# Two quarter products of a seven-product matrix multiply change places, in the MLPs of a transformer trunk

## The chip, the cores and the metric

The kernel runs on one core of a Trainium2 chip. The metric is the device time of one execution in microseconds (us). A core has five engines that work at the same time, each through its own queue of instructions in a fixed order, and that wait for one another by semaphores: TensorE (PE in the profile, with its weight loads shown as PEld), VectorE (DVE), ScalarE (ACT), GpSimd (POOL) and SyncE (SP, which issues nearly all of this kernel's loads).

## The reference

A trunk of two layers works on 512 tokens of width 1024, in float32. The first layer mixes tokens by stick-breaking attention beside a state-space model, the second by sparse attention. Behind each mixer stands an MLP with a residual and a layer norm, and only the two MLPs matter here:

```python
ALPHA = (2 * DEPTH) ** 0.25                      # DEPTH = 2
def sq_relu_mlp(x, w1, w2):                      # w1: 1024 x 4096, w2: 4096 x 1024
    return jnp.square(jax.nn.relu(x @ w1)) @ w2
x = layer_norm(ALPHA * x + sq_relu_mlp(x, mlp_w1[i], mlp_w2[i]), ln_ffn_g[i], ln_ffn_b[i])
```

## The kernel before

**Products of float32.** Each operand is split into a rounded part (`hi`, type fp32r, made by a cast on ACT) and the remainder (`lo`, made by a subtraction on DVE, for a few weights on POOL). Three matmuls, hi x hi, hi x lo and lo x hi, stand for one product of a 128 x 128 with a 128 x 512 piece.

**The MLP** (`mlp`, L205 to L271). Let h be the squared ReLU of x @ w1. It is made in blocks of 128 hidden columns, transposed, by `proj_fm` (L135): a load of 512 KB of w1 on SP, the cast L104 and the remainder L105 of these weights, 24 matmuls (L131 to L133), then on ACT the ReLU (L227) and the square (L228). Such a piece of work is called a w1 block here.

The product of h with w2 takes its 4096 hidden columns in four parts of 1024. The first three parts are the chunks; each is done by `down_chunk` (L273). The fourth part is done in the plain way (`mlp_block`). A chunk is a product of a 512 x 1024 matrix A (512 tokens by 1024 hidden columns of h) with a 1024 x 1024 matrix B (rows of w2). Each is cut in quarters. A11 and A21 are the first and the second 256 tokens of the chunk's first four h blocks (one tile, `hs[0]`), A12 and A22 those of its last four (`hs[1]`). B11, B12, B21 and B22 are 512 x 512 each, loaded from w2 as two pieces of 512 KB. Instead of eight quarter products the chunk makes seven, of sums and differences of quarters, in the manner of Strassen and Winograd; a quarter product's result goes by additions into one or more quarters of the residual x, or into a tile u that is added to three quarters at the end.

**One quarter product** (`product`, L302) takes two PSUM banks from a pool of four (`psb`). It makes the halves of its A operand (cast L298 on ACT, remainder L299 on DVE; tiles `whi` and `wlo` of the pool `self.wp`, which has four of each and shares them with the w1 blocks' weights), then of each of its two B pieces (L298, L299; `whi` and `wlo` of the MLP's own pool `hp`, four of each), and runs 24 matmuls (L311 to L313). Sums of B pieces are made by `combine` (L293, DVE), sums of A quarters by the lines L334, L345, L347 and L354 (DVE), results are added by L320 and L323 (DVE) or copied or added to u by L329 (ACT) and L331 (DVE).

**What stands between the products.** `down_chunk` is a generator. At each of its seven `yield`s the MLP issues one w1 block of the next chunk, and the eighth after the last. So in program order a w1 block follows each product, two of them stand at the end of a chunk, and the next chunk's first product comes right behind these two. The very first chunk of an MLP follows its own eight w1 blocks.

**What sets the order.** The program order is a wish. A planner simulates the program with estimated durations and writes each engine's queue from that; instructions whose operands are ready can pass others that wait. Buffers of a tag are handed out in rotation, and a load, a cast or a matmul that writes a buffer waits until the former tile in it has been read for the last time. Loads of B stand on SP's queue (L287) among those of the weights (L101).

**Names and lines of the steps below.** Before the change a chunk begins with the loads of B12 and B11, A21 + A22 (L334, written into A21), B12 - B11 (L293, written into B12), and the product of the two (L336), added to the quarters (1,1) and (0,1) of x. Then comes the w1 block, the loads of B22, and the product A11 x B11 (L341), added to the quarter (0,0) and gathered in u. Then follow (A12 - (A21 + A22 - A11)) x B22 (L348) and four more (L352, L356, L361, L363).

Of the kernel before, what the change touches and what calls it, by code (L numbers as in the profile page):

```python
# [11 lines left out]
ALU = mybir.AluOpType  # L12
# [23 lines left out]
class Trunk:  # L36
# [236 lines left out]
    def down_chunk(self, hp, w2, r0, hs, u, touched, last):  # L273

        nc, mm = self.nc, self.nc.tensor.matmul
        vec, act = nc.vector, nc.scalar
        a11, a21 = hs[0][:, :, 0:256], hs[0][:, :, 256:512]
        a12, a22 = hs[1][:, :, 0:256], hs[1][:, :, 256:512]  # L280

        def load(tag, j, n):
            ts = []
            for i in range(2):
                t = hp.tile([P, 1024], F32, tag=tag, bufs=2, name=self.nm(tag)).rearrange("p (k c) -> p k c", c=512)
                r = r0 + j * 512 + i * 256
                nc.sync.dma_start(t, w2[r:r + 256, n * 512:n * 512 + 512].rearrange("(k p) c -> p k c", p=P))  # L287
                ts.append(t)
            return ts

        def combine(out, x, y, op):
            for o, p, q in zip(out, x, y):
                vec.tensor_tensor(o, p, q, op)  # L293

        def halves(src, pool, c):
            hi = pool.tile([P, 1024], F32R, tag="whi", bufs=4, name=self.nm("whi")).rearrange("p (k c) -> p k c", c=c)
            lo = pool.tile([P, 1024], F32R, tag="wlo", bufs=4, name=self.nm("wlo")).rearrange("p (k c) -> p k c", c=c)
            act.copy(hi, src)  # L298
            vec.tensor_tensor(lo, src, hi.bitcast(F32), ALU.subtract)  # L299
            return hi, lo  # L300

        def product(a, b):  # L302
            pss = [self.psb.tile([P, 512], F32, tag="psb", name=self.nm("psb")) for _ in range(2)]
            ahi, alo = halves(a, self.wp, 256)
            for i in range(2):
                bhi, blo = halves(b[i], hp, 512)
                for t, ps in enumerate(pss):
                    tok = slice(t * P, (t + 1) * P)
                    for k in range(2):
                        lh, ll = ahi[:, 2 * i + k, tok], alo[:, 2 * i + k, tok]  # L310
                        mm(ps, lh, bhi[:, k, :], start=i + k == 0, stop=False)  # L311
                        mm(ps, lh, blo[:, k, :], start=False, stop=False)  # L312
                        mm(ps, ll, bhi[:, k, :], start=False, stop=i + k == 2)  # L313
            return pss

        def add(pss, row, col, op=ALU.add):
            for t, ps in enumerate(pss):
                xs = self.x[:, 2 * row + t, col * 512:col * 512 + 512]
                if (row, col, t) in touched:
                    vec.tensor_tensor(xs, xs, ps, op)  # L320
                else:
                    touched.add((row, col, t))
                    vec.scalar_tensor_tensor(xs, xs, ALPHA, ps, ALU.mult, op)  # L323

        def gather(pss):
            for t, ps in enumerate(pss):
                if ("u", t) not in touched:
                    touched.add(("u", t))
                    act.copy(u[:, t, :], ps)  # L329
                else:  # L330
                    vec.tensor_tensor(u[:, t, :], u[:, t, :], ps, ALU.add)  # L331

        b12, b11 = load("b12", 0, 1), load("b11", 0, 0)
        vec.tensor_tensor(a21, a21, a22, ALU.add)  # L334
        combine(b12, b12, b11, ALU.subtract)
        ps = product(a21, b12)  # L336
        add(ps, 1, 1)
        add(ps, 0, 1)
        yield
        b22 = load("b22", 1, 1)  # L340
        ps = product(a11, b11)  # L341
        add(ps, 0, 0)
        gather(ps)
        yield
        vec.tensor_tensor(a11, a21, a11, ALU.subtract)  # L345
        s4 = hp.tile([P, 4, 256], F32, tag="s4", bufs=1, name=self.nm("s4"))
        vec.tensor_tensor(s4, a12, a11, ALU.subtract)  # L347
        add(product(s4, b22), 0, 1)  # L348
        yield
        combine(b12, b22, b12, ALU.subtract)  # L350
        b21 = load("b21", 1, 0)
        gather(product(a11, b12))  # L352
        yield
        vec.tensor_tensor(a11, a22, a11, ALU.subtract)  # L354
        combine(b11, b12, b11, ALU.subtract)
        ps = product(a11, b11)  # L356
        add(ps, 1, 0)
        add(ps, 1, 1)
        yield
        combine(b22, b12, b21, ALU.subtract)  # L360
        add(product(a12, b21), 0, 0)  # L361
        yield
        add(product(a22, b22), 1, 0, ALU.subtract)  # L363
        if last:
            for row, col in ((0, 1), (1, 0), (1, 1)):
                xs = self.x[:, 2 * row:2 * row + 2, col * 512:col * 512 + 512]
                vec.tensor_tensor(xs, xs, u, ALU.add)
        yield
# [832 lines left out]
```

## Time and profile before

| | |
|---|---|
| median of 3 runs | 1206.27 us |
| lowest and highest run | 1199.74 and 1209.66 us |
| the profiled execution, its own time | 1203.52 us |
| its span, from first to last instruction | 1201.7 us |
| granted clock of TensorE, mean over the span | 0.972 of full |
| chunks of the first MLP (first matmul of each) | at 303.3, 391.5 and 479.9 us |
| chunks of the second MLP | at 891.4, 978.7 and 1067.0 us |

How to read the lines that follow. A group or a row names an engine, an operation and its line in the kernel, then the written tile, an arrow and the read tiles, shapes and a count (x6). Times are in us, in a timeline the first number is the start from the span's begin and the second the duration; square brackets hold the idle time of the engine just before and what ended it. `A <- B: 22.1, 6, 3.7` in a list of waits means that A waited for B for 22.1 us in all, in 6 places, the longest 3.7. Matmuls are pipelined: one starts before the modelled end of the one before it, so spacing is read from start to start. A chain of waits lists, going back from the end, what each step was released by; "issue" is a time in which nothing that the profile shows was waited for. The letter q behind an engine (SPq) is its sequencer, which issues loads. Several instructions of one group that follow each other are merged in one row with their count, whose duration then runs from the first to the last and includes what they waited.

### The profile page before, as it was taken

How to read it: one execution, taken by the hardware profiler on the slowest of the kernel's cores; microseconds unless marked ns; L12 is line 12 of the kernel's file. 1: busy time of each engine (PE TensorE's matmuls, PEld its weight loads, DVE VectorE, ACT ScalarE, POOL GpSimd, SP SyncE). 2: the span in 40 equal slices, each digit the busy share in tenths (PEclk: the TensorE clock that was granted, in tenths of full speed). 3: DMA queues.
4: the chain of work that ended last, by engine and by line, in shares of the span. 5: the costliest groups of instructions: out<-in, count | busy, mean ns of one | idle time of the engine just before them, and what ended most of it. 6: DMA issues, size and time to landing. Idle time of an engine off the chain costs nothing.

```text
span 1201.7 us, 15563 instructions
## 1 busy us (share of the span) xinstructions
PE 1125.3 (94%) x5860; PEld 934.5 (78%) x5860; DVE 842.7 (70%) x1255; ACT 533.6 (44%) x832; POOL 173.1 (14%) x201
## 2 busy tenths in 40 slices
PE   7989998999999998999999959998989989989997
PEld 6878776788787787888888847776978878878886
DVE  7997598673865865965568997549637667567736
ACT  5534486324543543554135437642334435445510
POOL 1044130410000000000021735324000000000001
PEclk9998999999899899999999979999999989999999
DMA  7535772930241341333056860034313414414101
GB/s 238 140 85 140 199 223 52 268 118 1 88 141 53 94 150 37 115 110 79 1 146 150 212 152 1 19 121 135 97 35 106 141 35 122 124 35 140 53 1 70
DMA packets 147306, 126.99 MB, mean 106 GB/s; under 512 B 24352, under 2 KB 115296, under 8 KB 147232
## 3 DMA queue, kind: packets, MB, share of 16 engines
q1 hardware_dynamic: 145552, 123.59, 36.1%
q10 hardware_dynamic: 1680, 2.41, 0.6%
q8 instruction: 46, 0.75, 0.3%
q14 instruction: 28, 0.23, 0.1%
HBM read 105.80 MB, written 5.37 MB: 93 GB/s over the span
## 4 chain that ended last, share of the span: by engine, by line
PE 77%; DVE 13%; DMA 4%; ACT 3%; issue 2%; SPq 1%; POOL 0%; POOLq 0%; DVEq 0%; ACTq 0%
PE psa L132 11%; PE psa L131 11%; PE psa L133 11%; PE psb L311 7%; PE psb L312 7%; PE psb L313 7%; PE pso L948 3%; PE psb L379 2%; PE psb L381 2%; PE psb L380 2%; PE pst L941 2%; DVE acc L1113 2%; DVE top L1112 2%; PE psb L840 2%; PE psb L842 1%
## 5 line engine op out<-in xcount | busy, mean ns | idle before, releaser
L132 PE MATMUL psa<-xlo,whi 128*128 128x512 f32 (+1 forms) x720 | 268.0, 373 | 0.0
L131 PE MATMUL psa<-xhi,whi 128*128 128x512 f32 (+1 forms) x720 | 267.0, 373 | 0.2 <-ACT xhi L202 0.2
L133 PE MATMUL psa<-xhi,wlo 128*128 128x512 f32 (+1 forms) x720 | 267.0, 371 | 0.0
L104 ACT CAST whi<-raw 128x1024 fp32r<-128x1024 f32 (+1 forms) x129 | 133.4, 1045 | 198.5 <-PE psa L132 115.0
L105 DVE TENSOR_TENSOR wlo<-raw,whi 128x1024 fp32r<-128x1024 f32 (+1 forms) x102 | 127.9, 1258 | 79.0 <-ACT whi L104 78.6
L311 PE MATMUL psb<-whi,whi 128*128 128x512 f32 x336 | 136.0, 405 | 22.1 <-ACT whi L298 22.1
L132 PEld LDWEIGHTS psa<-xlo,whi 128*128 128x128 f32 x720 | 136.5, 190 | 23.6 <-DVE xlo L203 0.4
L131 PEld LDWEIGHTS psa<-xhi,whi 128*128 128x128 f32 x720 | 135.8, 189 | 23.5 <-ACT xhi L202 0.5
L133 PEld LDWEIGHTS psa<-xhi,wlo 128*128 128x128 f32 x720 | 135.7, 188 | 23.1
L299 DVE TENSOR_TENSOR wlo<-b,whi 128x1024 fp32r<-128x1024 f32 x84 | 102.6, 1222 | 52.2 <-ACT whi L298 52.0
L312 PE MATMUL psb<-wlo,whi 128*128 128x512 f32 x336 | 134.8, 401 | 0.0
L313 PE MATMUL psb<-whi,wlo 128*128 128x512 f32 x336 | 133.1, 399 | 0.0
L298 ACT CAST whi<-b 128x1024 fp32r<-128x1024 f32 x84 | 88.4, 1052 | 55.8 <-PE psb L313 43.9
L311 PEld LDWEIGHTS psb<-whi,whi 128*128 128x128 f32 x336 | 66.0, 196 | 38.5 <-ACT whi L298 24.6
L105 POOL TENSOR_TENSOR wlo<-raw,whi 128x1024 fp32r<-128x1024 f32 x27 | 70.8, 2632 | 135.2 <-ACT whi L104 117.2
L184 POOL TENSOR_TENSOR rs<-rs,two 128x1 f32<-128x1 f32 x16 | 22.7, 1417 | 441.4 <-DVE rs L183 441.4
L313 PEld LDWEIGHTS psb<-whi,wlo 128*128 128x128 f32 x336 | 65.5, 195 | 14.3
L312 PEld LDWEIGHTS psb<-wlo,whi 128*128 128x128 f32 x336 | 65.7, 195 | 13.7
L293 DVE TENSOR_TENSOR b<-b,b 128x1024 f32<-128x1024 f32 x48 | 63.2, 1317 | 11.2 <-DMA b<-in_w_dram 10.3
L227 ACT ACTIVATE h<-psa 128x512 f32<-128x512 f32 x48 | 28.5, 594 | 80.6 <-PE psa L133 80.6
L334 DVE TENSOR_TENSOR h<-h,h 128x1024 f32<-128x1024 f32 x6 | 7.4, 1225 | 70.3 <-ACT h L228 70.3
L298 ACT CAST whi<-h 128x1024 fp32r<-128x1024 f32 x36 | 37.9, 1052 | 42.2 <-PE psb L312 34.4
(263 smaller groups left out, 2021.5 us busy)
## 6 DMA issues: line engine op xcount, KB each, us to landing
raw<-in_w_dram SPq DMA_DIRECT2D x80, 512.0 KB, 4.1
b<-in_w_dram SPq DMA_DIRECT2D x48, 512.0 KB, 4.4
raw<-in_w_in_dram SPq DMA_DIRECT2D x29, 512.0 KB, 4.4
raw<-in_w_out_dram SPq DMA_DIRECT2D x16, 512.0 KB, 4.9
qst<-hl SPq DMA_DIRECT2D x48, 128.0 KB, 3.8
kst<-hl SPq DMA_DIRECT2D x24, 256.0 KB, 4.5
gb<-in_ln_g_dram SPq DMA_DIRECT2D x4, 512.0 KB, 4.2
gb<-in_ln_b_dram SPq DMA_DIRECT2D x4, 512.0 KB, 5.1
```

What stands on the lines that cost most here:

```text
L104: nc.scalar.copy(hi[:, c], raw[:, c])
L105: (eng or nc.vector).tensor_tensor(lo[:, c], raw[:, c], hi[:, c].bitcast(F32), ALU.subtract)
L131: mm(ps, lhi, rhi, start=start, stop=False)
L132: mm(ps, lhi, rlo, start=False, stop=False)
L133: mm(ps, llo, rhi, start=False, stop=stop)
L293: vec.tensor_tensor(o, p, q, op)
L298: act.copy(hi, src)
L299: vec.tensor_tensor(lo, src, hi.bitcast(F32), ALU.subtract)
L311: mm(ps, lh, bhi[:, k, :], start=i + k == 0, stop=False)
L312: mm(ps, lh, blo[:, k, :], start=False, stop=False)
L313: mm(ps, ll, bhi[:, k, :], start=False, stop=i + k == 2)
L948: last = self.nc.tensor.matmul(po[64 * h:64 * h + 64, :], v[:, s, cols[h]:cols[h] + 64], wt[:, s, h, :], start=s == 0, stop=s == qb)
```

## The change

The product A11 x B11 comes first in each chunk: load of B11, product, addition, gathering, and the w1 block behind it. The load of B12, B12 - B11, A21 + A22, their product and its two additions follow as the second, with the w1 block behind them, and the load of B22 comes after that. All operands, all products and the other five products' order stay as they were.

```diff
-        b12, b11 = load("b12", 0, 1), load("b11", 0, 0)
+        b11 = load("b11", 0, 0)
+        ps = product(a11, b11)
+        add(ps, 0, 0)
+        gather(ps)
+        yield
+        b12 = load("b12", 0, 1)
+        combine(b12, b12, b11, ALU.subtract)
         vec.tensor_tensor(a21, a21, a22, ALU.add)
-        combine(b12, b12, b11, ALU.subtract)
         ps = product(a21, b12)
         add(ps, 1, 1)
         add(ps, 0, 1)
         yield
         b22 = load("b22", 1, 1)
-        ps = product(a11, b11)
-        add(ps, 0, 0)
-        gather(ps)
-        yield
         vec.tensor_tensor(a11, a21, a11, ALU.subtract)
         s4 = hp.tile([P, 4, 256], F32, tag="s4", bufs=1, name=self.nm("s4"))
         vec.tensor_tensor(s4, a12, a11, ALU.subtract)
```

## The prediction

> **What bounds the kernel now.** I began with the first part of the page, to see which engine fills the span.
>
> ```profile
> span 1201.7 us, 15563 instructions
> PE 1125.3 (94%) x5860; PEld 934.5 (78%) x5860; DVE 842.7 (70%) x1255; ACT 533.6 (44%) x832; POOL 173.1 (14%) x201
> ```
>
> PE is busy for 1125.3 of 1201.7 us. An order of work can win only what PE loses, which is its 76.4 us without a matmul and the time in which its matmuls run slowly. So the second view is the list of PE's waits, longest total first; this row is the top one.
>
> ```profile
> PE psb L311 <- ACT whi L298: 22.1, 6, 3.7
> ```
>
> L311 is the first matmul line of `product`, L298 the cast in `halves`. There are six waits for six chunks (three in each of the two MLPs), the longest 3.7 us, and 22.1/6 = 3.68, so all six are alike. The third view is the chain of waits around one of them, the second chunk of the first MLP.
>
> ```profile
> 387.55 0.24 PE psa L133
> 387.79 0.02 issue
> 387.81 0.61 ACT h L227
> 388.42 0.02 issue
> 388.44 0.64 ACT h L228
> 389.08 0.02 issue
> 389.10 1.24 DVE h L334
> 390.34 0.02 issue
> 390.36 1.05 ACT whi L298
> 391.41 0.04 issue
> 391.45 0.80 PE psb L311
> ```
>
> The last matmul of the w1 product (L133) ends; its block is rectified (L227) and squared (L228); then DVE forms A21+A22 (L334), ACT casts it (L298), and only then can the chunk's first product start. The last block of h is a part of A22, so this chain is real data dependence, with PE empty beside it. The fourth view, busy time by stretch, shows a second loss behind the pause. Columns: length, busy time of PE, PEld, DVE, ACT and POOL with counts, granted clock, DMA share, GB/s. The first six rows run from a chunk's first product matmul to the first matmul of its second product, 48 matmuls each (24 of the product, 24 of a w1 block; the count may be one off at an edge). The seventh is the next such pair.
>
> ```profile
> 303.28:316.89 13.61, 13.61 (x48) 11.00 (x49) 13.43 (x14) 5.85 (x6) 0.00 (x0) 0.80 0.27 77
> 391.45:405.31 13.86, 13.86 (x48) 11.23 (x49) 13.42 (x14) 5.85 (x6) 0.00 (x0) 0.78 0.26 76
> 479.88:492.29 12.41, 12.41 (x49) 10.17 (x50) 12.38 (x13) 5.85 (x6) 0.00 (x0) 0.88 0.30 86
> 891.42:904.08 12.66, 12.66 (x48) 10.17 (x49) 12.63 (x13) 5.84 (x6) 0.00 (x0) 0.87 0.30 84
> 978.65:992.45 13.80, 13.80 (x48) 11.17 (x49) 13.42 (x14) 5.85 (x6) 0.00 (x0) 0.78 0.27 76
> 1067.02:1079.64 12.62, 12.62 (x49) 10.33 (x50) 12.59 (x13) 5.85 (x6) 0.00 (x0) 0.88 0.29 83
> 316.89:327.77 10.88, 10.88 (x49) 9.01 (x48) 8.85 (x9) 6.23 (x9) 0.00 (x0) 1.00 0.41 114
> ```
>
> PE is busy all through these rows, yet the same 48 matmuls take 12.41 to 13.86 us behind a pause, at a granted clock of 0.78 to 0.88, and 10.88 us at clock 1.00, 0.227 us apiece. So each chunk loses twice: the pause, and the slow clock after it.
>
> **Part 1: A11 x B11 first, the gain.** What does the new first product need? The product reads A11 and B11. A11 is the first 256 tokens of the chunk's first four h blocks, so it waits for the fourth block, not the eighth. ACT's timeline shows both in the stretch that makes the second chunk's operands.
>
> ```profile
> 351.08 0.64 ACT L228 ACTIVATE h<-h 128x512 f32<-128x512 f32 x1
> ...
> 363.33 1.05 ACT L298 CAST whi<-b 128x1024 fp32r<-128x1024 f32 x1 [0.73 <-PE psb L313]
> 365.82 1.06 ACT L104 CAST whi<-raw 128x1024 fp32r<-128x1024 f32 x1 [1.44 <-PE psb L312]
> ```
>
> The fourth block is squared by 351.72, 36 us before the w1 products end. B's first piece for the coming product is cast at 363.33 already. The cast at 365.82, the weights of the chunk's last w1 block, waited for a matmul of the sixth product: the `whi` tag has four buffers in each pool, handed out in program order, so a cast waits for the last use of the tile four places back. For the first product's A, four places back are the weights of the w1 block that follows the sixth product, and 24 matmuls of 0.227 behind 365.8 those are free, at 371.3. The cast of A11 can thus run from there, 1.05 us as at 363.33, and its fp32r remainder behind it, done by 374, against 387.6 when PE wants them. B11 needs no subtraction, one step less than B12-B11, so its pieces are no later than those cast now.
>
> The pause then goes. Its price is start to start, because the ends of matmuls are modelled:
>
> ```profile
> 387.38 0.39 PE L133 MATMUL psa<-xhi,wlo 128*128 128x512 f32 x1
> 391.45 0.80 PE L311 MATMUL psb<-whi,whi 128*128 128x512 f32 x1 [3.68 <-ACT whi L298]
> ```
>
> 391.45 - 387.38 is 4.07; less one matmul of 0.227 it is 3.84 us, times six 23.1 us. The slow clock goes with it: the six rows sum to 78.96 us, and six at 10.88 make 65.28, so 13.7 us. Together **36.8 us**. Bounds: 23.1 if the slow clock somehow stayed, 36.8 if PE never pauses; I take the upper, since the clock is at 1.00 once PE has run on for a while (seventh row).
>
> **Part 2: A21+A22 and B12-B11 second, the new cover.** L334, the two L293 subtractions, the cast and remainder of A21 and the B12 halves now stand behind a product and a w1 block: 10.88 us of PE work. From the chain, the way from the last w1 matmul to the cast's end is 391.41 - 387.79 = 3.6 us, and the remainder, one more DVE pass over such a tile like L334 below, adds 1.2 us, 4.8 in all. So 6 us are spare, and I cost the move at nothing. If the cover were gone, the old 3.84 and its slow clock would be back.
>
> ```profile
> 340.35 1.23 DVE L293 TENSOR_TENSOR b<-b,b 128x1024 f32<-128x1024 f32 x1 [2.39 <-DMA b<-in_w_dram]
> 376.93 1.06 ACT L298 CAST whi<-b 128x1024 fp32r<-128x1024 f32 x1 [1.67 <-PE psb L313]
> 389.10 1.22 DVE L334 TENSOR_TENSOR h<-h,h 128x1024 f32<-128x1024 f32 x1 [7.85 <-ACT h L228]
> ```
>
> B12-B11 is finished at 341.6 now; the second product's last B piece is cast at 376.93, so this subtraction has 35 us to spare and may come one product later. DVE stands idle 7.85 us ahead of L334, behind which it then does the remainders of A21, of the next w1 weights and of A11. Of these, A11's and the weights' move into that idle time. ACT's two copies of the product into u (first chunk), DVE's two adds into x and two into u come 10.88 us earlier than they did; they read a finished product, and four banks serve two products, so none holds PE.
>
> Does the chunk as a whole still fit? This row is one chunk, from its first product to the next chunk's.
>
> ```profile
> 391.45:479.88 88.43, 84.74 (x361) 69.63 (x361) 60.22 (x62) 38.95 (x46) 0.00 (x0) 0.96 0.31 95
> ```
>
> 360 matmuls at 0.227 are 81.6 us; 60.22 us of DVE are 74% of that, 38.95 of ACT 48%. PE stays the bound.
>
> **Part 3: the loads.** B11's two loads come ahead of B12's, B12's move behind the first product and its w1 weights, B22's two move behind one more w1 weight load. All are on SP's queue. The landing time of such loads is the last number of the second fence, in us:
>
> ```profile
> 322.15 4.00 SPq L287 DMA_DIRECT2D b<-in_w_dram  x2
> 330.09 0.37 SPq L101 DMA_DIRECT2D raw<-in_w_dram  x1
> 333.03 4.00 SPq L287 DMA_DIRECT2D b<-in_w_dram  x2
> ...
> 354.79 5.03 SPq L287 DMA_DIRECT2D b<-in_w_dram  x2
> 362.72 45.96 SPq L101 DMA_DIRECT2D raw<-in_w_dram  x5
> ```
>
> ```profile
> b<-in_w_dram SPq DMA_DIRECT2D x48, 512.0 KB, 4.4
> ```
>
> In order, these are next chunk's B12, B11 and B22, each issued when its buffer came free. Even right behind the first issue of the 362.72 row B12 would be in by 362.7 + 0.4 + 4.4 = 367.5, some 30 us before its product. B22 in that place would be in as early, and its product, the third, starts two products and two w1 blocks after 387.6, at 409.4. I take nothing for the loads, with 0 and the wait of rival D as bounds.
>
> **Sum.** The profiled execution took 1203.5 us (span 1201.7 and 1.8 around it); less 36.8 it is 1166.7. The median of the runs, 1206.3, is 0.2% above the profiled one; from it the same gain gives 1169.5. I forecast **1168 us**.
>
> **Rivals.**
>
> A, the second product comes late: the DVE queue is the tightest near the chunk's start. In the second chunk's row it works 13.42 us where 10.88 will be there. If all of that had to be done before the third product, 2.54 us a chunk would stay, 15.2 in all: 1168 + 15 = 1183. For it: DVE is in order, and L345 and L347 queue there for the third product. Against: 7.85 us idle just ahead. Its pauses would be well below 3.68, and I add no slow clock, because a pause of 1.97 had none (clock 1.00 in the second row); with it the time would be 1183 + 13.7 = 1197.
>
> ```profile
> 245.75 1.09 PE L199 MATMUL pst<-ident,x 128*128 128x128 f32 x8 [1.97 <-DVE x L189]
> 243.00:250.00 7.00, 5.03 (x31) 4.20 (x29) 6.97 (x11) 3.56 (x6) 2.18 (x2) 1.00 0.00 0
> ```
>
> The page "TensorE: Matmul & The Clock Gate" of the Trainium skill, Part 1, states that an idle window of about 3.4 us halves the clock until PE has been busy for as long again. By that rule, too, pauses of 2.54 us would cost only themselves, 1183 and not 1197.
>
> B, the pause is a lack of buffers. Then the first product, whichever it is, gets its `whi` tile only when the last w1 block is done, the pause of 3.68 stays, and the time is 1204 to 1206. For it: casts do wait for buffers (365.82, above). Against: the chain shows no buffer, but L227, L228 and L334. The page "Perfetto Trace Analysis" of the Trainium skill, under the optimization strategy, says that one gap repeating on the busy engine can mean too little SBUF or PSUM; by that rule the order would win nothing. This trace speaks against it here.
>
> C, the change doesn't do what it says: a planner writes each engine's order from simulated times and may place the cast of A11 behind that of A21. No gain, 1204 to 1206. Against: it already hands out buffers in program order, and that order now has A11 first.
>
> D, slower: B12's loads come to stand behind all the weight loads that hold SP from 362.72 to 408.68. Then the second product starts at 408.7 + 4.4 + 1.2 (L293) + 1.1 (L298) = 415.4 instead of 387.6 + 10.9 = 398.5. That is 16.9 us, in the four chunks that are not loaded ahead, 67.6 us, and some 2.3 us of slow clock each: 1168 + 77 = 1245. The change is lost once wait and slow clock in each of the four pass 36.8/4 = 9.2 us. Against: every pair of b is issued ahead of that block, and B12's buffer is free first of all.
>
> **Numbers.** Forecast 0.80, A 0.09, B 0.04, C 0.03, D 0.04. Unknown in the forecast itself: the slow clock after equal pauses cost 1.5 to 3.0 us, so the kernel's other slow stretches may shift by a few us, and single runs of before lie from 6.5 below to 3.4 above the median. That makes 1158 to 1178, and with A the range is **1158 to 1184**, which leaves out B, C, D and the edges, some 0.15. A measurement tells 1% (12 us) from no change. Faster by over 1% are the forecast and A, 0.89; within 1% B and C, 0.07; slower D, 0.04.
>
> **What would show it.** PE's wait list has no row of L311 behind L298; the twin stretches behind the w1 blocks are 10.88 us at clock 1.00; A11's cast stands before the last L228 of its chunk; L334 runs beside the first product; chunks are 81.6 us apart. I am wrong if L311 waits at the second product's start (A, D), or if the first still waits behind L298 (B, C).

## The result, and the profile after

The changed kernel takes 1166.07 us in the median of four runs (1164.96 to 1169.02), the kernel before 1206.23 us beside it. The ratio is 0.9677, 95% interval 0.9632 to 0.9722: faster by 3.2%; the medians differ by 40 us. The forecast was 1168 us in a range of 1158 to 1184, with 0.89 for faster by over 1%.

First the page of the changed kernel, whose span is 38.2 us shorter.

```profile
span 1163.5 us, 15569 instructions
PE 1108.7 (95%) x5860; PEld 923.6 (79%) x5860; DVE 841.5 (72%) x1255; ACT 532.4 (46%) x832; POOL 173.1 (15%) x201
```

The engines do the same work; PE is busy for 16.6 us less with the same 5860 matmuls, since fewer of them run at the slow clock. Next, the top of PE's list of waits after.

```profile
PE psl L1136 <- DVE pst L1143: 14.6, 1, 14.6
PE psu L131 <- ACT whi L104: 6.9, 1, 6.9
```

The row of L311 behind L298, which led this list with 22.1 us, is gone, and no wait of the MLP's chunks has come in its place. Busy time by stretch shows the other loss: these are the first product and the w1 block behind it in the first MLP's three chunks, the twins of three of the six rows in the prediction (length; busy PE, PEld, DVE, ACT, POOL; clock).

```profile
299.31:310.19 10.88, 10.88 (x50) 9.01 (x49) 9.33 (x9) 7.18 (x10) 0.00 (x0) 1.00 0.00 0
380.91:391.79 10.88, 10.88 (x50) 9.01 (x49) 9.33 (x10) 6.21 (x8) 0.00 (x0) 1.00 0.00 0
462.51:473.39 10.88, 10.88 (x50) 9.01 (x49) 9.33 (x10) 6.21 (x8) 0.00 (x0) 1.00 0.00 0
```

Each takes 10.88 us at clock 1.00, as do the second MLP's three, and their starts are 81.6 us apart. Where did the 38.2 us come from? The same view by stage, first of the kernel before, then of the changed one: the first MLP from its w1 blocks to its fourth part, the attention between the MLPs, and the second MLP with the last normalisations ahead of it.

```profile
265.79:563.00 297.21, 286.16 (x1272) 237.26 (x1273) 194.62 (x198) 137.10 (x167) 0.53 (x1) 0.97 0.29 88
563.00:830.90 267.90, 245.50 (x1509) 202.75 (x1507) 194.63 (x450) 115.45 (x262) 95.21 (x113) 0.97 0.40 106
830.91:1150.14 319.23, 307.49 (x1425) 257.16 (x1425) 211.59 (x221) 144.85 (x176) 4.44 (x3) 0.97 0.28 84
```

```profile
265.65:544.11 278.46, 278.46 (x1273) 232.40 (x1274) 194.01 (x198) 136.72 (x167) 0.53 (x1) 1.00 0.31 94
544.11:810.40 266.29, 244.10 (x1510) 201.44 (x1508) 194.61 (x450) 115.44 (x262) 95.15 (x113) 0.97 0.39 107
810.38:1111.85 301.47, 300.78 (x1424) 253.22 (x1425) 210.95 (x221) 144.59 (x176) 4.44 (x3) 0.99 0.30 89
```

The two MLPs gave 18.75 and 17.76 us, 36.5 together, where 36.8 were forecast; in the first one PE is now busy for all of its 278.46 us. The attention gave 1.6 us that the change has nothing to do with. There a stretch at the slow clock is gone, before and after:

```profile
629.46 0.81 PE L1077 MATMUL psx<-kist,qist 96*128 96x256 f32 x3 [1.86 <-issue]
629.00:634.00 5.00, 4.54 (x25) 4.32 (x26) 3.10 (x6) 1.65 (x6) 0.00 (x0) 0.66 1.05 267
```

```profile
610.12 0.59 PE L1078 MATMUL psx<-kist,qist 96*128 96x256 f32 x3 [1.41 <-issue]
610.10:615.10 5.00, 4.99 (x40) 4.85 (x41) 3.28 (x7) 2.62 (x9) 0.00 (x0) 1.00 1.04 258
```

Last, how near the new cover is to its end. In the second chunk of the changed kernel these are ACT's and DVE's rows for A11 (first two), for the sum A21+A22 and its halves, and PE's row at the second product's start; the last w1 block's ReLU starts at 381.11.

```profile
364.56 1.05 ACT L298 CAST whi<-h 128x1024 fp32r<-128x1024 f32 x1 [3.43 <-PE psa L132]
365.65 1.23 DVE L299 TENSOR_TENSOR wlo<-h,whi 128x1024 fp32r<-128x1024 f32 x1 [3.08 <-ACT whi L298]
...
381.11 0.60 ACT L227 ACTIVATE h<-psa 128x512 f32<-128x512 f32 x1 [4.17 <-PE psa L133]
382.40 1.23 DVE L340 TENSOR_TENSOR h<-h,h 128x1024 f32<-128x1024 f32 x1 [4.33 <-ACT h L228]
383.82 1.05 ACT L298 CAST whi<-b 128x1024 fp32r<-128x1024 f32 x1 [1.46 <-PE psb L313]
384.79 1.05 ACT L298 CAST whi<-h 128x1024 fp32r<-128x1024 f32 x1
388.39 1.22 DVE L299 TENSOR_TENSOR wlo<-h,whi 128x1024 fp32r<-128x1024 f32 x1
391.79 0.39 PE L311 MATMUL psb<-whi,whi 128*128 128x512 f32 x1
```

A11 is cast 15 us and its remainder done 14 us ahead of the first product at 380.91, released by a w1 matmul as forecast. The sum's cast ends 4.7 us behind the last w1 matmul and its remainder 8.5 us behind it; the sum is ready at 383.63, then ACT casts a piece of B first, and from the end of the sum's cast (385.84) to 388.39 DVE does other things. That matters below.

### The profile page after: what moved, and what is told of

Its sections match the earlier page's. It is cut to its first block, busy times and chain, and to the rows that moved or that the text cites. A ratio compares the mean times of both kernels' runs of the same rounds, so it can differ in the third digit from the quotient of the medians.

```text
span 1163.5 us, 15569 instructions
## 1 busy us (share of the span) xinstructions
PE 1108.7 (95%) x5860; PEld 923.6 (79%) x5860; DVE 841.5 (72%) x1255; ACT 532.4 (46%) x832; POOL 173.1 (15%) x201
## 4 chain that ended last, share of the span: by engine, by line
PE 80%; DVE 12%; DMA 3%; issue 2%; ACT 2%; SPq 1%; POOLq 0%; DVEq 0%; ACTq 0%
PE psa L133 11%; PE psa L132 11%; PE psa L131 11%; PE psb L313 7%; PE psb L311 7%; PE psb L312 7%; PE pso L949 3%; PE psb L382 3%; PE psb L381 3%; PE psb L380 2%; PE pst L942 2%; DVE acc L1114 2%; DVE top L1113 2%; PE psb L841 2%; PE psb L842 2%
## 5 line engine op out<-in xcount | busy, mean ns | idle before, releaser
L133 PEld LDWEIGHTS psa<-xhi,wlo 128*128 128x128 f32 x720 | 135.8, 189 | 23.1
L131 PEld LDWEIGHTS psa<-xhi,whi 128*128 128x128 f32 x720 | 135.0, 188 | 23.1 <-ACT xhi L202 0.5
L299 DVE TENSOR_TENSOR wlo<-b,whi 128x1024 fp32r<-128x1024 f32 x84 | 102.5, 1221 | 43.0 <-ACT whi L298 42.8
L311 PE MATMUL psb<-whi,whi 128*128 128x512 f32 x336 | 130.7, 389 | 0.0
L312 PE MATMUL psb<-wlo,whi 128*128 128x512 f32 x336 | 130.7, 389 | 0.0
L313 PE MATMUL psb<-whi,wlo 128*128 128x512 f32 x336 | 129.7, 389 | 0.0
L298 ACT CAST whi<-b 128x1024 fp32r<-128x1024 f32 x84 | 88.3, 1051 | 42.0 <-PE psb L313 30.2
L312 PEld LDWEIGHTS psb<-wlo,whi 128*128 128x128 f32 x336 | 63.1, 188 | 13.2
L313 PEld LDWEIGHTS psb<-whi,wlo 128*128 128x128 f32 x336 | 63.1, 188 | 13.1
L311 PEld LDWEIGHTS psb<-whi,whi 128*128 128x128 f32 x336 | 63.1, 188 | 13.0
L298 ACT CAST whi<-h 128x1024 fp32r<-128x1024 f32 x36 | 38.0, 1054 | 54.0 <-PE psb L312 34.0
L299 DVE TENSOR_TENSOR wlo<-h,whi 128x1024 fp32r<-128x1024 f32 x36 | 43.9, 1220 | 14.0 <-ACT whi L298 13.5
L841 PE MATMUL psb<-whi,xhi 128*128 128x512 f32 x128 | 51.5, 410 | 0.8 <-DVE x L848 0.6
```

Source lines behind the costliest of these rows:

```text
L131: mm(ps, lhi, rhi, start=start, stop=False)
L133: mm(ps, llo, rhi, start=False, stop=stop)
L841: nc.tensor.matmul(ps, chi[:, k, tok], whi, start=i == 0, stop=False)
```

## The experiments

All ratios are to the kernel before, run on the same chip in the same job, with their 95% interval.

**The loads alone.** The new order of the loads with the old order of the products (B12 stays ahead of the first product, which needs it):

```diff
-        b12, b11 = load("b12", 0, 1), load("b11", 0, 0)
+        b11 = load("b11", 0, 0)
+        b12 = load("b12", 0, 1)
...
-        b22 = load("b22", 1, 1)
         ps = product(a11, b11)
         add(ps, 0, 0)
         gather(ps)
         yield
+        b22 = load("b22", 1, 1)
```

> The products keep the order of the kernel before; only the loads change as in the change (B11 ahead of B12, B22 behind the second product). My theory, that the whole gain is the pause before A21+A22 and the slow clock after it, expects no change: six waits of L311 behind L298 of 3.68 us each and 1200 to 1210 us. The rival, that a part of the gain comes from the other order of the loads, expects less than 1195 us.

Measured: 1204.0 us, ratio 1.000 (0.998 to 1.002). The wait is the old one, word for word:

```profile
PE psb L311 <- ACT whi L298: 22.1, 6, 3.7
```

So the order of the loads in the program neither gives nor takes anything. The traces say why. In the stretch that loads the second chunk, SP issues the four pairs of B pieces, the first piece of each within 0.1 us of the end of the remainder (L299) that reads its buffer last, at 322.15, 333.03, 343.92 and 354.79 us before, at 324.05, 334.93, 345.81 and 356.69 in this run, at 315.98, 326.32, 337.30 and 348.09 in the changed kernel. In all three they come in the order of the buffers, B12 first. The changed order of the program did not reach SP's queue there.

**The first MLP alone.** `down_chunk` takes the new order where `self.n_mlp == 1`, else the old one.

> The change is made in the first MLP alone. My theory adds up by chunks: three pauses of 3.84 us and the slow clock of those three chunks (2.73, 2.98 and 1.53 us) are 18.8 us, so about 1187 us, with three waits of L311 left, all behind 850 us of the span. The rival, that the chunks' gains depend on each other or come from elsewhere (the attention between the MLPs, the tail), expects 1168 or 1206 us, or three waits with a time off by more than 6 us.

Measured: 1184.4 us, ratio 0.9835 (0.981 to 0.986), 19.9 us by the ratio where 18.8 were expected. Three waits are left:

```profile
PE psb L311 <- ACT whi L298: 11.0, 3, 3.7
```

The gain adds up by chunks. One of the three pauses left, though as long as the others, has no slow clock behind it (more of that under the clock rule):

```profile
873.97:884.86 10.89, 10.89 (x48) 8.93 (x49) 10.86 (x11) 5.86 (x6) 0.00 (x0) 1.00 0.34 96
```

**The cover taken away.** A11 x B11 stays first, but one w1 block earlier, so that the product of the sums follows the chunk's last w1 block directly:

```diff
             for c in range(3):
-                ups = up_raw(c + 1) if c < 2 else itertools.chain(up_split(6), up_split(7))
-                got = []
-                for _ in self.down_chunk(hp, w2, c * 1024, hs, u, touched, c == 2):
+                down = self.down_chunk(hp, w2, c * 1024, got[-1], u, touched, c == 2)
+                next(down)
+                got += ups
+                ups = up_raw(c + 1) if c < 2 else itertools.chain(up_split(6), up_split(7))
+                got = []
+                for _ in down:
                     got += itertools.islice(ups, 1)
-                got += ups
-                hs = got[-1]
+                got += itertools.islice(ups, 1) if c < 2 else ups
```

(The first chunk's w1 blocks are issued up to the seventh ahead of the loop in the same way.)

> A11 x B11 is still first, but one w1 block earlier, ahead of the chunk's last w1 block, so that the product of the sums follows that block directly, as the first product did before the change. My theory, that the gain is the cover of 10.88 us between the last w1 block and the product of the sums, expects the pause of 3.84 us and the slow clock back six times, at the second product: 1200 to 1209 us. The rival, that A11 x B11 first is better in itself (fewer steps, earlier casts), expects 1163 to 1172 us.

Measured: 1203.9 us, ratio 0.9996 (0.998 to 1.001). PE waits as before, now at the second product (L313 is that kernel's number for L311, L300 for L298):

```profile
PE psb L313 <- ACT whi L300: 22.1, 6, 3.7
```

All of the gain is gone although A11 x B11 is still first and all buffers are the same. So what pays is the work that stands between the last w1 block and the product of the sums. This also settles rival B: with the same four buffers the pause comes and goes with the order alone.

**A shorter pause in the kernel before.** The sum in two instructions:

```diff
-        vec.tensor_tensor(a21, a21, a22, ALU.add)
+        for k in (slice(0, 3), slice(3, 4)):
+            vec.tensor_tensor(a21[:, k], a21[:, k], a22[:, k], ALU.add)
```

> The kernel before, with A21+A22 made in two instructions, three blocks of h and then the last one, so that only a quarter of the sum is left behind the last block. A 128x1024 pass takes 1.23 us and a 128x512 one 0.68, so a quarter should take about 0.4: the pause falls from 3.84 to about 3.0 us start to start, 5 us in six. If the slow clock needs an idle time of a full 3.4 us (the rule of the page), it goes as well, 13.7 us more: about 1187 us. If it needs only little activity over some window, it stays: about 1201 us. I hold the first for likelier.

Measured: 1195.3 us, ratio 0.9922 (0.989 to 0.995), between the two expectations. List of waits, then the stretches from the chunks' first product to their second:

```profile
PE psb L311 <- ACT whi L298: 17.3, 6, 2.9
```

```profile
302.79:315.14 12.35, 12.35 (x48) 10.13 (x49) 12.32 (x13) 5.84 (x6) 0.00 (x0) 0.88 0.30 85
388.90:399.94 11.04, 11.04 (x48) 9.04 (x49) 11.01 (x12) 5.87 (x6) 0.00 (x0) 1.00 0.34 95
...
1057.28:1071.22 13.94, 13.94 (x48) 11.21 (x49) 13.45 (x14) 5.84 (x6) 0.00 (x0) 0.78 0.26 75
```

All pauses are alike, 2.88 us. The clocks behind them are 0.88, 1.00 and 0.78 in the rows shown and 0.79, 0.87 and 1.00 in those left out. So an idle time shorter than 3.4 us can bring the slow clock, and whether it does changes from one equal pause to the next. The two effects are apart here: the pauses shrank by 22.1 - 17.3 = 4.8 us, the rest of the 9.4 us (0.78% of 1203.9) is slow clock that was spared.

**A longer pause in the kernel before.** Two more DVE passes behind the sum (A22 is subtracted and added again), 1.25 us each:

```diff
         vec.tensor_tensor(a21, a21, a22, ALU.add)
+        for _ in range(1):
+            vec.tensor_tensor(a21, a21, a22, ALU.subtract)
+            vec.tensor_tensor(a21, a21, a22, ALU.add)
```

> The kernel before with two more DVE passes behind A21+A22: each pause is 2.5 us longer, 6.2 instead of 3.68. If the slow clock's price belongs to the clock's return alone, as I hold, it stays at 1.5 to 3.0 us a pause and the time grows by the pauses only, six times 2.5 = 15 us: 1217 to 1223 us. If the price grows with the pause (2.3 us for 3.68, so 3.9 for 6.2), it is 10 us more: 1229 us or so.

Measured: 1221.2 us, ratio 1.0131 (1.011 to 1.015), 15.8 us more, with six waits of 6.2 us:

```profile
PE psb L311 <- ACT whi L298: 37.2, 6, 6.2
```

The pauses grew by 37.2 - 22.1 = 15.1 us, which leaves 0.7 for the slow clock, where the interval of the ratio is 2.8 us to either side. Its price belongs to each return, not to the length of the pause.

**Half the cover.** The first two products in a row, the two w1 blocks behind them:

```diff
         gather(ps)
-        yield
         b12 = load("b12", 0, 1)
...
         add(ps, 0, 1)
         yield
+        yield
         b22 = load("b22", 1, 1)
```

> The changed kernel without a w1 block between its first two products: both stand in a row, two w1 blocks behind them. The cover falls from 10.88 to 5.44 us. My theory says that the way to A21 takes 3.6 us to the end of the cast and 4.8 to the end of the remainder, both less than 5.44: no wait at the second product, 1163 to 1170 us. The rival A of the prediction, that DVE's queue is what limits the chunk's start, expects a pause of 1 us or more in each chunk, 1172 us or more.

Measured: 1177.7 us, ratio 0.977 (0.975 to 0.979). My theory said no wait, and there is one of about 1.15 us in four chunks (and of 0.55 in the two others, behind DVE's L299):

```profile
PE psb L311 <- ACT whi L298: 4.6, 4, 1.2
```

```profile
381.81:396.14 14.33, 13.17 (x57) 10.36 (x56) 12.78 (x13) 8.56 (x10) 0.00 (x0) 1.00 0.05 11
```

(The second is the stretch around such a wait; the clock stays at 1.00.) DVE's queue of this kernel says why:

```profile
383.30 1.23 DVE L339 TENSOR_TENSOR h<-h,h 128x1024 f32<-128x1024 f32 x1 [5.59 <-ACT h L228]
...
389.29 1.22 DVE L299 TENSOR_TENSOR wlo<-h,whi 128x1024 fp32r<-128x1024 f32 x1
...
390.57 0.50 PE L311 MATMUL psb<-whi,whi 128*128 128x512 f32 x1 [1.16 <-ACT whi L298]
```

The remainder of A21 ends at 390.51, 8.5 us behind the last w1 block, not 4.8, and PE goes on at 390.57. (The view names ACT: its cast of the third product's s ends at 390.51 too, and the next matmul in PE's queue, an L311, waits for ACT. So this row can't tell the two apart; in the two first chunks the view names the remainder.) These waits, 6.7 us from start to start, are most of the 10.6 us by which the span is longer than the changed kernel's. So the spare time that I had given to the cover was wrong, and the next four runs measure it.

**Longer ways to A21 in the changed kernel.** The same additional passes behind the sum: four, eight, and then two.

> The changed kernel with four more DVE passes (subtract and add A22 again, twice) behind A21+A22, each some 1.25 us when it depends on the one before: 5.0 us more on the way to A21. My theory of 6 us to spare expects no wait at the second product, 1163 to 1171 us, although DVE works 30 us more in all. The rival A, that less is spare because of DVE's queue, expects pauses and 1172 us or more.

Measured: 1207.4 us, ratio 1.0026 (1.001 to 1.004). The whole gain is lost.

> The same with eight more passes, 10.0 us. The way to the end of the cast is then 13.6 us against a cover of 10.88: a pause of about 2.7 us at the second product of each chunk, six times 16 us, and after the experiment with the split sum, where pauses of 2.88 us were followed by the slow clock in four of six, some 6 to 9 us of slow clock: 1187 to 1193 us, with six waits of L311 behind L298 again. If more than 6 us are spare (the planner finds other work for PE), it is below 1180; if less, above 1200.

Measured: 1237.3 us, ratio 1.0265 (1.024 to 1.029). Both are far above what I expected. Their waits, four passes first:

```profile
PE psb L311 <- ACT whi L298: 24.8, 6, 4.5
```

```profile
PE psb L311 <- ACT whi L298: 55.9, 6, 10.0
```

In the run with four, DVE's rows between the sum (L340) and ACT's cast of it:

```profile
388.35 1.23 DVE L340 TENSOR_TENSOR h<-h,h 128x1024 f32<-128x1024 f32 x1 [4.33 <-ACT h L228]
389.61 1.23 DVE L342 TENSOR_TENSOR h<-h,h 128x1024 f32<-128x1024 f32 x1
390.87 1.23 DVE L299 TENSOR_TENSOR wlo<-b,whi 128x1024 fp32r<-128x1024 f32 x1
392.01 0.68 DVE L320 TENSOR_TENSOR x<-x,psb 128x512 f32<-128x512 f32 x1
...
400.08 1.22 DVE L343 TENSOR_TENSOR h<-h,h 128x1024 f32<-128x1024 f32 x1
...
401.33 1.04 ACT L298 CAST whi<-h 128x1024 fp32r<-128x1024 f32 x1 [2.13 <-DVE h L343]
```

Between the passes (L340, L342, L343) stand a remainder of B and an addition of the first product; three more additions, one more remainder and two B differences follow in the part left out. Counted from the last block's ReLU, the cast ends 402.37 - 387.06 = 15.3 us behind the last w1 block instead of 4.7: five microseconds of work became ten and a half of delay. The theory was then that the order of DVE's queue makes the pause, not the length of the cover, and two runs were to tell.

> The changed kernel with two more dependent DVE passes behind A21+A22, 2.5 us by themselves. With four of them the cast of A21 ended 15.4 us behind the last w1 matmul instead of 4.8, because the planner put other DVE work between the passes. My new theory, that the way to A21 is stretched by DVE's queue, expects about half of that, some 5 us: the cast ends at about 10 us, just inside the cover of 10.88, the remainder at 11 to 13: 1166 to 1178 us, short waits at the second product or none. If each pass simply costs its 1.25 us in front of PE (the straight line through four and eight passes), the pause is 2.0 us and the time 1180 to 1190 us. If 6 us are spare, as the prediction said, it is 1163 to 1171 us without any wait.

Measured: 1173.9 us, ratio 0.974 (0.971 to 0.977). The wait is now for the remainder alone, about 1 us in four chunks:

```profile
PE psb L313 <- DVE wlo L299: 3.8, 4, 1.0
```

That is the first of the three expectations. The cast ends 8.5 us behind the last w1 block and the remainder 13.1, so two passes, 2.5 us by themselves, put the remainder back by 4.6 us. The last run has four passes again, with DVE's queue ordered by hand:

```diff
-        ps = product(a11, b11)
-        add(ps, 0, 0)
-        gather(ps)
+        ps0 = product(a11, b11)
+        vec.tensor_tensor(a21, a21, a22, ALU.add)
+        for _ in range(2):
+            vec.tensor_tensor(a21, a21, a22, ALU.subtract)
+            vec.tensor_tensor(a21, a21, a22, ALU.add)
         yield
...
         ps = product(a21, b12)
+        made = self.alo_ins                      # A21's remainder, L299
+        with self.tc.issue_after(made):
+            add(ps0, 0, 0)
+            gather(ps0)
...
+        with self.tc.issue_after(made):
+            add(product(s4, b22), 0, 1)
```

(In the same way A11's new value, L346 of the changed kernel, and the last B difference are queued behind `made`.)

> The changed kernel with four more passes behind A21+A22, as in the run that took 1207 us, but with DVE's queue ordered by hand: the passes and A21's remainder stand in a row, and the additions of the first product, the third product's remainders, A21+A22-A11 and the last B difference are queued behind them. The passes cost the same, DVE's total work is the same, and the cover is the same. My new theory, that the queue's order and not the cover's length made the pause, expects the cast at 1.3 + 6.25 + 1.05 = 8.6 us and the remainder at 9.8 us behind the last w1 matmul, inside 10.88: no wait of L311, 1163 to 1173 us. The rival, that the cover is too short for 5 us more, expects the pauses of 4.5 us again and some 1207 us.

Measured: 1179.6 us, ratio 0.979 (0.976 to 0.983), 28 us less than the run with the same passes in the planner's order, though above what I expected. The second product does not wait any more:

```profile
382.82 0.60 ACT L227 ACTIVATE h<-psa 128x512 f32<-128x512 f32 x1 [4.18 <-PE psa L133]
...
390.41 1.05 ACT L298 CAST whi<-h 128x1024 fp32r<-128x1024 f32 x1 [1.10 <-DVE h L339]
391.50 1.23 DVE L299 TENSOR_TENSOR wlo<-h,whi 128x1024 fp32r<-128x1024 f32 x1 [1.12 <-ACT whi L298]
407.64 1.22 DVE L299 TENSOR_TENSOR wlo<-s,whi 128x1024 fp32r<-128x1024 f32 x1
```

The cast ends 8.6 us and the remainder 9.9 us behind the last w1 block, as expected, inside the 10.88. What I had missed is the last row: the third product's remainder (s) has moved back with everything that was queued behind, to 408.9, and the waits for such a remainder are new (L314 is that kernel's number for L313):

```profile
PE psb L314 <- DVE wlo L299: 6.9, 6, 1.8
```

The last of them, 1.81 us long, brought the slow clock back in the profiled execution:

```profile
1067.80:1072.80 5.00, 5.00 (x15) 3.95 (x16) 5.00 (x5) 1.05 (x1) 0.00 (x0) 0.66 0.72 214
```

## Why the prediction was right, and where it was not

**The gain** (Part 1) came as its two terms: the pauses are gone, 23.1 us start to start, and so is the slow clock, 13.7 us; the MLPs measured 36.5 for 36.8. The shorter and the longer pause price the two terms apart. A11's operands were ready 14 us ahead, as worked out from the buffers' rotation.

**The new cover** (Part 2) hid the moved work, so its cost of nothing was right, but the spare time of 6 us behind it was wrong. I took the way to A21 as 3.6 us to the cast's end and 4.8 to the remainder's; the trace has 4.7 and 8.5. The failed step: I added up the chain's own instructions as though DVE and ACT served it at once. One cast of B stands ahead on ACT, which makes 1.1 of the 3.7 us, and other work on DVE holds the remainder for 2.6 us more. So 2.2 us were spare (389.61 to 391.79), not 6. Two more passes already cost a wait, four cost the whole gain.

**The loads** (Part 3) cost nothing, but not for the reason given: in the second chunk's loads, which the traces show, their order did not change. What B12's loads would cost behind a w1 block's weights stays untested.

**Rivals.** A named the right resource: DVE's queue is what decides as soon as the way grows. It did not decide in the changed kernel, where DVE works 9.33 of the 10.88 us. Of its reading that small pauses bring no slow clock, the 1.15 us pauses (clock 1.00) agree, but the 1.81 us wait of the last run does not (clock 0.66). B is refuted by the run without cover. C did not happen: the cast of A11 stands where program order put it. D did not happen: SP issued the pairs of B in the old order, B12 first, ahead of the block of weight loads.

**The clock rule.** Pauses of 2.88 us brought the slow clock in four of six places, and in the attention one of 1.86 us did (clock 0.66). The traces show what decides. In each of the twelve profiled executions, one per kernel, the granted clock is either 1.00 or 0.50, and it changes only at times that lie whole steps of 3.41 us apart (the end of the record aside); where this grid lies differs from one execution to the next. Here are two of the equal pauses of the split sum, cut along its grid, the pause from 386.0 to 388.9 and the one from 470.8 to 473.7:

```profile
384.23:387.64 3.41, 1.79 (x8) 1.13 (x7) 0.29 (x1) 1.23 (x2) 0.00 (x0) 1.00 0.00 0
387.65:391.06 3.41, 2.15 (x9) 1.72 (x10) 2.30 (x3) 3.25 (x4) 0.00 (x0) 1.00 0.00 0
469.57:472.98 3.41, 1.25 (x6) 0.71 (x4) 0.43 (x1) 1.60 (x3) 0.00 (x0) 1.00 0.00 0
472.98:476.39 3.41, 2.69 (x6) 2.15 (x7) 2.71 (x3) 3.41 (x4) 0.00 (x0) 0.50 0.02 5
```

The grid divides the first pause, PE is busy for 1.79 and 2.15 us of the two steps, and the clock stays at 1.00. Most of the second pause falls into one step, in which PE is busy for 1.25 us, and the next step is slow. The pauses in the chunks of all runs agree: a step at full clock with PE idle for 1.96 us or more was always followed by a slow one, one with 1.77 or less never (of the two between, one was, at 1.81, and one wasn't, at 1.91); a slow step was followed by full clock where PE was idle for 0.52 us or less, and never where it was idle for 0.62 or more. Where a pause falls on the grid is chance, so equal pauses differ, and the price of 1.5 to 3.0 us is what PE's matmuls lose in the slow time that is left when they start again.

The page "TensorE: Matmul & The Clock Gate" of the Trainium skill (Part 1) ties the slow clock to an idle window of about 3.4 us, which runs freely. The traces agree on the window and its length, but the window need not be idle as a whole: 1.96 of its 3.41 us were enough.

The kernel's total also has 1.6 us of luck in it, the slow stretch that the attention lost: the wait there was 1.41 instead of 1.86 us in that execution.

## What to carry to other kernels

When PE's only waits are for an operand made from the last thing that PE itself produced, look for a piece of work that needs nothing of it and put that in front; the gain is the pause and the slow clock behind it, here 23 and 14 us. Check the cover by the whole queue of each engine on the operand's way, not by the sum of the chain's own instructions: here 5 us more of work in that way became 10.5 us of delay. A pause that can't be removed may still be worth shortening, since the slow clock came behind a pause of 2.88 us in four of six places, and behind one of 3.68 us in 20 of 21 (four runs).

## What was not expected of the hardware

Equal pauses of 2.88 us were followed by clocks of 1.00 or of 0.78 to 0.88 in the same execution, and one of 1.86 us by 0.66: what counts is how long PE was idle within one step of a 3.41 us grid, at which alone the clock changed. In the kernel before, pauses of 3.68 and of 6.2 us cost nearly the same slow clock, each in all six places (13.7 and about 14.4 us).
